# The down projections of a two-layer encoder on one core: sixteen instead of twelve of 22 k blocks as Strassen products

## The chip, the core and the metric

The kernel runs on one core of a Trainium2 chip. A core has five engines with a queue of instructions each: TensorE (PE, matmuls; PEld is its weight load), VectorE (DVE), ScalarE (ACT), GpSimd (POOL), and SyncE (SP), which issues the DMAs. They wait for each other by semaphores only. The metric is the device time of one execution in microseconds; three runs of the kernel before took 1592.32 to 1599.11, median 1592.86.

## The reference, cut to what matters

Two layers, each a token mixer, a cross-attention and a SwiGLU feed-forward; each of the three adds to the stream and normalises it.

```python
D_MODEL, SEQ, FFN_HIDDEN = 1024, 512, 2816

def swiglu(x, w_gu, w_down):
    gate, up = jnp.split(x @ w_gu, 2, axis=-1)
    return (jax.nn.silu(gate) * up) @ w_down

# in each layer, last
ff = swiglu(x, ffn_w_gu[layer], ffn_w_down[layer])
x = layer_norm(DEEPNORM_ALPHA * x + ff, ln_g[layer, 2], ln_b[layer, 2])
```

The change touches `(...) @ w_down` alone: 512 tokens by 2816 hidden features times 2816 by 1024.

## The kernel before, in words

**Three matmuls for one.** All is float32, but the matmuls run on float32r operands. Each operand is split into a high part (a cast on ACT) and a low part (the value minus the high part, on DVE or POOL), and a product is three matmuls: high by high, high by low, low by high. For weights the parts are `whi` and `wlo` (`chunk`, L131; `pair`, L543), for the hidden features `hi`/`lo`, and `fh`/`fl` for sums of them.

**The feed-forward** (`ffn`, L454). `fast_units` (L370) makes the 22 blocks of 128 hidden features, `raws[0]` to `raws[21]`, each 128 features by 512 tokens. `split` (L462) makes `hi` and `lo` of one. `fast_down` (L503) multiplies them by the down weights, in two ways that add into the same result:

- *Direct* (`mul`, L525): k blocks 0 to 9 in five pairs. One weight row of 128x1024 holds two k blocks by 512 output features; for one pair and one of the four token blocks that is 6 matmuls of 128x512. For the first half of the output features this is 120 matmuls into the four `pj` banks, ahead of the products; for the second half 120 matmuls behind them (L677 on).
- *Strassen* (L533 to L666): k blocks 10 to 21 in two halves `K[0]`, `K[1]` of six, cut by c into three groups of two. Tokens, output features and k are cut in two, and seven products p1 to p7 of sums and differences take the place of eight. A step is one (p, c): 12 matmuls of 128x512 (L661). Before it stands its preparation (`prep`, L601): a difference of weight rows (`diff`, L557), the split of it (`pair`), a sum of hidden blocks (`sums`, L579, tiles `sr`, `s3`), and its split (`tokens` L563, `whole` L572). `pair` of p3 and p2 and the sum `s3` of p7 are POOL's, the other sums, differences and low parts DVE's, the casts ACT's.

**What sets the order.** The steps are p1 and p5 in turn for each c; then p6, p3 and p7, each for all c; then p4 and p2 in turn for each c. `queue` holds the preparations in that order, with a step number; `upto` emits them some steps ahead of the matmuls. A layer that records the program then settles the order on each engine. Tiles come from rings: `raw` has 2 buffers, `whi`/`wlo` 5, `fh`/`fl` 6, `s3` 2. An operation that writes a tile waits until the reader of the buffer's last content is done. The tiles that hold the transposed stream (`mxh`, `mxl` here) serve as store for the weight rows b12 and b22 while the products run.

**The end of it.** When the two banks of a token half are done, `add` (L515) adds them to x on DVE; then `norm` (L303) normalises a token block: on DVE statistics, two passes of 512 columns twice, with a square root by POOL between. The output goes to the next layer or out.

Of the kernel before, what the change touches and what calls it, by code (L numbers as in the profile page):

```python
# [10 lines left out]
F32 = mybir.dt.float32  # L11
# [35 lines left out]
class Trunk:  # L47
# [406 lines left out]
    def ffn(self, l):  # L454
        nc, a = self.nc, self.a
        parts, raws = [], []
        self.halves = []

        def slot(j, dt):
            return self.kvblk(dt) if 8 <= j < 16 else self.part(dt=dt)  # L460

        def split(pool, n):  # L462
            j = len(parts)
            hi = pool.tile([P, S], F32R, tag="hi", bufs=n, name=self.nm("hi"))
            lo = self.kvblk(F32R) if 10 <= j < 18 else self.part()
            self.split(raws[j][0], hi, lo, raws[j][1])
            parts.append((hi, lo))

        def act(j, g, u, sign):

            s = slot(j, F32)
            nc.scalar.activation(g[1], g[0], AF.Silu)
            nc.vector.tensor_tensor(s, g[1], u, ALU.mult)
            raws.append((s, sign))

        with self.phase("pre") as pre:
            with self.phase("gu") as pool:
                new = self.tiles(pool)
                first = self.tproj_halves([a["gu"][l, j] for j in (0, HB, 1, HB + 1)])
                T = self.fast_tokens(lambda t: pool.tile([P, 4, 256], F32R, tag=t, name=self.nm(t)))  # L480
                for j in range(2):
                    pg, pu = first[2 * j:2 * j + 2]
                    act(j, (pg, new("o", 2, w=1024)[:, :512]), pu, 1)

                def unit(j):
                    def raw():
                        r = []
                        for x in (j, HB + j):
                            p = (self.wp, pool)[j % 2]
                            r.append(p.tile([P, 1024], F32, tag="raw", bufs=2, name=self.nm("raw")))  # L490
                            nc.sync.dma_start(r[-1], a["gu"][l, x])
                        return r
                    return {"raw": raw, "tag": ("at", "pj")[j % 2],
                            "done": lambda o: act(j, (o[:, :512], o[:, :512]), o[:, 512:], -1)}

                ready = []
                two = lambda: [split(pre, 6) for _ in range(2)]
                load = lambda: ready.append(self.chunk(a["down"][l][0, len(ready)]))
                self.fast_units([unit(j) for j in range(2, HB)], T, new, [load, two, load, two, two])
            with self.phase("down") as pool:  # L500
                self.fast_down(l, raws, parts, lambda: split(pool, 4), ready, pool)

    def fast_down(self, l, raws, parts, split, ready, pool):  # L503

# [1 line left out]
        mm = nc.tensor.matmul  # L508
        wsrc, idx = a["down"][l], 3 * l + 2
        last = idx + 1 == self.stop  # L510
        K = [[raws[10 + 6 * h + k][0] for k in range(6)] for h in range(2)]
        tok = slice(0, 256), slice(256, 512)
        res = []

# [19 lines left out]
        with self.phase("fast") as fp:  # L534
            new = self.tiles(fp)
            xt = [self.xtp.tile([P, KB, S], F32R, tag=t, name=self.nm("m" + t)).rearrange("p k s -> p (k s)")
                  for t in ("xh", "xl")]
            home = [x[:, i * 1024:(i + 1) * 1024].bitcast(F32) for x in xt for i in range(4)] + [new("t", 1, w=1024)]
            b12, b22, tt = home[:3], home[3:6], home[6:]
            sr = [new(f"sr{c}", 1) for c in range(3)]  # L540
            w, f, row = {}, {}, {}

            def pair(key, src, eng=None):  # L543
# [10 lines left out]
            def fetch(dst, h, i):  # L554
                nc.sync.dma_start(dst, wsrc[h, i])
# [2 lines left out]
                nc.vector.tensor_tensor(out, x, y, ALU.subtract)  # L558

            def form():  # L560
                return new("fh", 6, dt=F32R), new("fl", 6, dt=F32R)

            def tokens(key, src):  # L563
                hi, lo = form()
# [22 lines left out]
                return lambda k: sr[c][:, tok[k]]  # L587

            def b11(c):
                row[c] = stream(0, 5 + c)  # L590
                pair(("p1", c), row[c])

            def b21(c):
                row[c] = stream(0, 8 + c)
                diff(tt[c], row[c], tt[c])

            def s3(c):
                row["s3", c] = new("s3", 2)
                sums(row["s3", c], block(0, c, 0), block(0, c, 1), ALU.subtract, nc.gpsimd)

            prep = {  # L601
# [12 lines left out]
                "p4": lambda c: [lambda: b21(c), lambda: pair(("p4", c), tt[c]), lambda: whole(c)],  # L614
                "p2": lambda c: [lambda: pair(("p2", c), row[c], nc.gpsimd)],
            }
            steps = [(p, c) for c in range(3) for p in ("p1", "p5")]
            steps += [(p, c) for p in ("p6", "p3", "p7") for c in range(3)]
            steps += [(p, c) for c in range(3) for p in ("p4", "p2")]
            rest = b22 + b12[:2]  # L620
            early = [lambda: ready.append(self.chunk(wsrc[0, 2])), split, lambda: ready.append(self.chunk(wsrc[0, 3])),
                     split, lambda: [fetch(b12[c], 1, 5 + c) for c in range(3)], split,
                     lambda: ready.append(self.chunk(wsrc[0, 4])), split]
            queue = [(0, g) for g in early]
            for s, (p, c) in enumerate(steps):
                queue += [(s, g) for g in prep[p](c)]
                if s == 1:
                    queue += [(s, lambda: [fetch(b22[c], 1, 8 + c) for c in range(3)])]
                if (p, c) == ("p4", 0):
                    queue += [(s, lambda: [fetch(r, 1, i) for i, r in enumerate(rest)])]  # L630
            queue += [(len(steps) + i, lambda i=i: pair(i, rest[i])) for i in range(5)]

            def upto(s):
                while queue and queue[0][0] <= s:
                    queue.pop(0)[1]()

            pj = [self.bank("pj") for _ in range(TB)]
            for i in range(5):
                while len(ready) <= i or len(parts) < 2 * i + 2:
                    queue.pop(0)[1]()  # L640
                for t in range(TB):
                    mul(pj[t], t, i, ready[i], i == 0)
                    queue.pop(0)[1]()
                if i == 1:
                    for t in range(TB):
                        x = pool.tile([P, D], F32, tag=f"x{t}", name=self.nm("x"))
                        nc.sync.dma_start(x, self.xd[t * P:(t + 1) * P, :])
                        res.append((x, self.sp.tile([P, 2, 6], F32, tag="st", bufs=4, name=self.nm("st"))))
# [3 lines left out]
            to = {"p1": (0, 0, True, False), "p5": (2, 1, True, False), "p6": (0, 1, True, False),  # L652
                  "p7": (2, 0, True, False), "p4": (2, 0, False, True), "p2": (0, 0, False, True)}
            for s, (p, c) in enumerate(steps):
                upto(s + (4 if s >= 15 else 3))
                for t in range(2):
                    for k in range(2):
                        (fh, fl), tk, wk = f[p, c][k], slice(t * P, (t + 1) * P), slice(k * 512, (k + 1) * 512)
                        hi, lo = w[p, c]
                        for n, (l_, r) in enumerate(((fh, hi), (fh, lo), (fl, hi))):  # L660
                            mm(out[p][t], l_[:, tk], r[:, wk], start=c == k == n == 0 and p in ("p1", "p5"),  # L661
                               stop=k == 1 and n == 2, skip_group_check=True)
                if c == 2 and p in to:
                    t0, h, first, done = to[p]
                    for t in range(2):
                        add(out[p][t], t0 + t, h, first, done)  # L666
            upto(len(steps) + 5)
        with self.phase("ln") as lp:
# [5 lines left out]
            else:  # L674
                xd = self.dp.tile([S, D], F32, tag="xd", bufs=2, name=self.nm("xd"))
                self.new_xt()
            for ts, turns in (((0, 1), ()), ((2,), (3,)), ((3,), (2,))):  # L677
                for i in range(5):
                    for t in ts:
                        mul((y + z)[t], t, i, w[i], False)  # L680
                    if i in turns and not last:
# [755 lines left out]
```

## Time and profile before

| What | us |
|---|---|
| median of three runs (lowest, highest) | 1592.86 (1592.32, 1599.11) |
| the profiled execution; its span from first to last instruction | 1595.57; 1593.9 |
| busy in the span: PE, DVE, ACT, POOL | 1561.3, 1163.3, 785.4, 262.1 |
| products of layer 0, from 707.90 to 766.70 | 58.8 |
| last matmul of layer 1's down projection begins; the span ends | 1585.47; 1593.9 |

The mean granted clock of PE is 0.996 of full speed. Times of rows are from the start of the span. A row of a timeline has the start, the time taken, engine, line, operation, tile written <- tiles read, shapes, the count of equal instructions in it, and in brackets the engine's idle time before it with what ended it. Layer 0's down projection lies at 676 to 796 us, layer 1's at 1468 us to the end.

### The profile page before, as it was taken

To read this page: it belongs to the slowest core of one execution; us is meant where nothing else is said; L and a number is where in the kernel's file an instruction comes from. 1 tells how busy PE (TensorE), PEld (TensorE's weight loads), DVE (VectorE), ACT (ScalarE), POOL (GpSimd) and SP (SyncE) were. 2 spreads that over 40 slices of the span, in tenths; PEclk is the share of its full clock that TensorE was granted. 3 is DMA by queue.
4 is the path that set the end of the run, shared out by engine and by line. 5 is a ranking of instruction groups with operands and counts; after the bars stand their busy time and mean duration, and the time that the engine had idled before them with its cause. 6 is when DMAs were issued, how large, how long until landed. Compare 5 with 4: busy or idle time off the path is not lost.

```text
span 1593.9 us, 24998 instructions
## 1 busy us (share of the span) xinstructions
PE 1561.3 (98%) x9668; PEld 1375.4 (86%) x9668; DVE 1163.3 (73%) x1892; ACT 785.4 (49%) x1465; POOL 262.1 (16%) x263
## 2 busy tenths in 40 slices
PE   8999999999999999999999999989999999999997
PEld 7877887898899999988898977767988999999886
DVE  4684445475499989898766588776745998988986
ACT  4684455244255555445245566663442655554450
POOL 0012000221220000014131144232212100000151
PEclk9999999999999999999999999999999999999999
DMA  5432343442333333353254433403413333333531
GB/s 166 141 98 75 101 145 126 171 135 76 134 120 119 106 101 103 103 211 93 80 181 132 131 88 93 132 27 119 146 53 146 119 120 103 104 103 102 198 93 66
DMA packets 59415, 185.89 MB, mean 117 GB/s; under 512 B 7680, under 2 KB 7840, under 8 KB 59296
## 3 DMA queue, kind: packets, MB, share of 16 engines
q1 hardware_dynamic: 59296, 184.30, 35.7%
q8 instruction: 76, 1.25, 0.3%
q14 instruction: 43, 0.35, 0.1%
HBM read 167.47 MB, written 12.60 MB: 113 GB/s over the span
## 4 chain that ended last, share of the span: by engine, by line
PE 35%; DVE 6%; ACT 3%; POOL 2%; DMA 2%; issue 2%; SPq 0%; POOLq 0%; DVEq 0%; ACTq 0%
PE pj L143 3%; PE pj L145 3%; PE pj L144 3%; PE at L661 3%; PE pj L416 2%; PE pj L417 2%; PE at L531 2%; PE pj L418 2%; PE pj L531 2%; PE at L416 2%; PE at L417 2%; PE at L418 2%; PE at L143 2%; PE at L144 2%; PE at L145 2%
## 5 line engine op out<-in xcount | busy, mean ns | idle before, releaser
L137 ACT CAST whi<-raw 128x1024 fp32r<-128x1024 f32 (+2 forms) x158 | 159.3, 1009 | 194.8 <-PE pj L144 67.2
L138 DVE TENSOR_TENSOR wlo<-raw,whi 128x1024 fp32r<-128x1024 f32 (+2 forms) x142 | 170.3, 1202 | 110.6 <-ACT whi L137 104.1
L143 PE MATMUL pj<-xh,whi 128*128 128x512 f32 (+1 forms) x640 | 228.0, 356 | 0.0
L145 PE MATMUL pj<-xh,wlo 128*128 128x512 f32 (+1 forms) x640 | 216.9, 339 | 0.6 <-DVE wlo L138 0.6
L144 PE MATMUL pj<-xl,whi 128*128 128x512 f32 (+1 forms) x640 | 216.5, 338 | 0.0
L397 ACT CAST whi<-sump 128x512 fp32r<-128x512 f32 x160 | 97.6, 621 | 113.3 <-issue 64.4
L143 PEld LDWEIGHTS pj<-xh,whi 128*128 128x128 f32 x640 | 120.7, 189 | 15.7 <-issue 5.2
L144 PEld LDWEIGHTS pj<-xl,whi 128*128 128x128 f32 x640 | 120.7, 189 | 14.7 <-issue 3.8
L145 PEld LDWEIGHTS pj<-xh,wlo 128*128 128x128 f32 x640 | 120.4, 188 | 14.8 <-DVE wlo L138 0.8
L401 DVE TENSOR_TENSOR wlo<-sump,whi 128x512 fp32r<-128x512 f32 x160 | 107.7, 688 | 13.3 <-ACT whi L397 13.1
L397 ACT CAST whi<-raw 128x512 fp32r<-128x512 f32 x120 | 72.2, 617 | 32.2 <-PE at L417 14.8
L581 POOL TENSOR_TENSOR s<-kv 128x256 f32<-128x256 f32 x12 | 14.6, 1235 | 439.5 <-DVE o L435 434.8
L401 DVE TENSOR_TENSOR wlo<-raw,whi 128x512 fp32r<-128x512 f32 x120 | 81.2, 688 | 0.5
L220 POOL TENSOR_SCALAR s<-s 128x1 f32<-128x1 f32 x56 | 26.0, 464 | 310.8 <-DVE s L306 167.9
L416 PE MATMUL at<-xh,whi 128*128 128x256 f32 x240 | 67.8, 283 | 2.6 <-DVE o L431 2.6
L416 PE MATMUL pj<-xh,whi 128*128 128x256 f32 x240 | 68.3, 285 | 1.3 <-DVE o L431 1.3
L417 PE MATMUL pj<-xl,whi 128*128 128x256 f32 x240 | 67.9, 283 | 0.0
L417 PE MATMUL at<-xl,whi 128*128 128x256 f32 x240 | 67.9, 283 | 0.0
L418 PE MATMUL at<-xh,wlo 128*128 128x256 f32 x240 | 67.8, 283 | 0.0
L138 POOL TENSOR_TENSOR wlo<-raw,whi 128x1024 fp32r<-128x1024 f32 x16 | 38.3, 2392 | 179.6 <-ACT whi L137 179.6
L418 PE MATMUL pj<-xh,wlo 128*128 128x256 f32 x240 | 67.8, 282 | 0.0
L143 PE MATMUL pj<-whi,part 128*128 128x512 f32 x144 | 59.5, 413 | 0.0
(396 smaller groups left out, 4849.5 us busy)
## 6 DMA issues: line engine op xcount, KB each, us to landing
raw<-gu SPq DMA_DIRECT2D x88, 512.0 KB
raw<-down SPq DMA_DIRECT2D x22, 512.0 KB
xd<-x SPq DMA_DIRECT2D x40, 256.0 KB
x<-xd SPq DMA_DIRECT2D x20, 512.0 KB
raw<-wk SPq DMA_DIRECT2D x16, 512.0 KB
raw<-wv SPq DMA_DIRECT2D x16, 512.0 KB
raw<-wq SPq DMA_DIRECT2D x16, 512.0 KB
raw<-wo SPq DMA_DIRECT2D x16, 512.0 KB
```

Source lines behind the costliest of these rows:

```text
L137: nc.scalar.copy(hi[:, :w], raw[:, :w])
L138: (eng or self.lo_eng).tensor_tensor(lo[:, :w], raw[:, :w], hi[:, :w].bitcast(F32), ALU.subtract)
L143: mm(out, lh, rh, start=first, stop=False)
L144: mm(out, lh, rl, start=False, stop=False)
L145: mm(out, ll, rh, start=False, stop=last)
L397: nc.scalar.copy(n[p, "w"][0], n[p])
L401: nc.vector.tensor_tensor(lo, n[p], hi.bitcast(F32), ALU.subtract)
L416: mm(out, hi[:, c], th[k], start=first, stop=False, skip_group_check=True)
L417: mm(out, hi[:, c], tl[k], start=False, stop=False, skip_group_check=True)
L418: mm(out, lo[:, c], th[k], start=False, stop=k == 3, skip_group_check=True)
L531: mm(bank, s[:, tk], w[:, c], start=first and j == n == 0, stop=j == 1 and n == 2, skip_group_check=True)
L661: mm(out[p][t], l_[:, tk], r[:, wk], start=c == k == n == 0 and p in ("p1", "p5"), stop=k == 1 and n == 2, skip_group_check=True)
```

## The change

Sixteen k blocks instead of twelve go through the seven products, so there are four groups c and 28 steps of 12 matmuls instead of 21. Six k blocks (0 to 5) stay direct, 72 matmuls ahead of the products and 72 behind, instead of 120 each. Their six splits are all made at the end of `fast_units`; four more that `fast_down` made are gone. `fh`/`fl` have 5 pairs of buffers instead of 6 and `s3` has one instead of two; there are four scratch tiles `t` of 1024 columns for the weight differences instead of one (two others were in `mxl`). All weights are read once, as before.

```diff
-                self.fast_down(l, raws, parts, lambda: split(pool, 4), ready, pool)
+                self.fast_down(l, raws, parts, ready, pool)
...
-        K = [[raws[10 + 6 * h + k][0] for k in range(6)] for h in range(2)]
+        K = [[raws[6 + 8 * h + k][0] for k in range(8)] for h in range(2)]
...
-            home = [x[:, i * 1024:(i + 1) * 1024].bitcast(F32) for x in xt for i in range(4)] + [new("t", 1, w=1024)]
-            b12, b22, tt = home[:3], home[3:6], home[6:]
-            sr = [new(f"sr{c}", 1) for c in range(3)]
+            home = [x[:, i * 1024:(i + 1) * 1024].bitcast(F32) for x in xt for i in range(4)]
+            home += [new(f"t{c}", 1, w=1024) for c in range(4)]
+            b12, b22, tt = home[:4], home[4:8], home[8:]
+            sr = [new(f"sr{c}", 1) for c in range(4)]
...
-                return new("fh", 6, dt=F32R), new("fl", 6, dt=F32R)
+                return new("fh", 5, dt=F32R), new("fl", 5, dt=F32R)
...
-                row["s3", c] = new("s3", 2)
+                row["s3", c] = new("s3", 1)
...
-            steps = [(p, c) for c in range(3) for p in ("p1", "p5")]
-            steps += [(p, c) for p in ("p6", "p3", "p7") for c in range(3)]
-            steps += [(p, c) for c in range(3) for p in ("p4", "p2")]
-            rest = b22 + b12[:2]
-            early = [lambda: ready.append(self.chunk(wsrc[0, 2])), split, lambda: ready.append(self.chunk(wsrc[0, 3])),
-                     split, lambda: [fetch(b12[c], 1, 5 + c) for c in range(3)], split,
-                     lambda: ready.append(self.chunk(wsrc[0, 4])), split]
+            steps = [(p, c) for c in range(4) for p in ("p1", "p5")]
+            steps += [(p, c) for p in ("p6", "p3", "p7") for c in range(4)]
+            steps += [(p, c) for c in range(4) for p in ("p4", "p2")]
+            rest = b22[:3]
+            early = [lambda: ready.append(self.chunk(wsrc[0, 2])), lambda: [fetch(b12[c], 1, 3 + c) for c in range(4)]]
...
-            for i in range(5):
-                while len(ready) <= i or len(parts) < 2 * i + 2:
+            for i in range(3):
+                while len(ready) <= i:
...
-            for ts, turns in (((0, 1), ()), ((2,), (3,)), ((3,), (2,))):
-                for i in range(5):
+            for ts, turns in (((0, 1), ()), ((2,), (2,)), ((3,), (2,))):
+                for i in range(3):
```

The order on POOL, layer 0, from the first `s3` (named `s_...`) to the last, before. `wlo` read from `mxh` or `mxl` is p3's low part; an `s3` is two rows.

```order
L581 TENSOR_TENSOR s_1349_7644<-kv_5788 128x256
L581 TENSOR_TENSOR s_1349_7644<-kv_5921 128x256
L581 TENSOR_TENSOR s_1354_7668<-kv_6052 128x256
L581 TENSOR_TENSOR s_1354_7668<-kv_6185 128x256
L546 TENSOR_TENSOR wlo_7576<-mxh_7211,whi_7575 128x1024
L546 TENSOR_TENSOR wlo_7598<-mxl_7212,whi_7597 128x1024
L581 TENSOR_TENSOR s_1359_7692<-kv_6316 128x256
L546 TENSOR_TENSOR wlo_7620<-mxl_7212,whi_7619 128x1024
L581 TENSOR_TENSOR s_1359_7692<-kv_6449 128x256
```

And in the same place in the changed kernel:

```order
L582 TENSOR_TENSOR s_1356_7666<-part_5260 128x256
L582 TENSOR_TENSOR s_1356_7666<-part_5393 128x256
L547 TENSOR_TENSOR wlo_7576<-mxl_7212,whi_7575 128x1024
L547 TENSOR_TENSOR wlo_7598<-mxl_7212,whi_7597 128x1024
L547 TENSOR_TENSOR wlo_7620<-mxl_7212,whi_7619 128x1024
L547 TENSOR_TENSOR wlo_7644<-mxl_7212,whi_7643 128x1024
L582 TENSOR_TENSOR s_1361_7690<-kv_5524 128x256
L582 TENSOR_TENSOR s_1361_7690<-kv_5657 128x256
L582 TENSOR_TENSOR s_1366_7714<-kv_5788 128x256
L582 TENSOR_TENSOR s_1366_7714<-kv_5921 128x256
L582 TENSOR_TENSOR s_1371_7738<-kv_6052 128x256
L582 TENSOR_TENSOR s_1371_7738<-kv_6185 128x256
```

Before, two `s3` were made ahead of everything and the third stood around the last `wlo` of p3; now one stands ahead, then the four `wlo` of p3, then the other three `s3`.

The order on DVE, layer 0, from the first `fl` of an `s3` to the second low part of p7, before. `x` is the stream, `mxh` holds b12.

```order
L155 SCALAR_TENSOR_TENSOR fl_7652<-s_1349_7644,fh_7651 128x512
L558 TENSOR_TENSOR mxl_7212<-raw_7715,mxl_7212 128x1024
L558 TENSOR_TENSOR mxl_7212<-raw_7763,mxl_7212 128x1024
L155 SCALAR_TENSOR_TENSOR fl_7676<-s_1354_7668,fh_7675 128x512
L519 SCALAR_TENSOR_TENSOR x_7306<-x_7306,at_7435 128x512
L546 TENSOR_TENSOR wlo_7648<-mxh_7211,whi_7647 128x1024
L519 SCALAR_TENSOR_TENSOR x_7309<-x_7309,at_7436 128x512
L155 SCALAR_TENSOR_TENSOR fl_7700<-s_1359_7692,fh_7699 128x512
L546 TENSOR_TENSOR wlo_7672<-mxh_7211,whi_7671 128x1024
```

In the changed kernel, from the first low part of p7 to the last `fl` of an `s3`; `t_...` is the scratch for p4's weights:

```order
L547 TENSOR_TENSOR wlo_7670<-mxh_7211,whi_7669 128x1024
L155 SCALAR_TENSOR_TENSOR fl_7650<-sr_1268_7220,fh_7649 128x512
L155 SCALAR_TENSOR_TENSOR fl_7674<-s_1356_7666,fh_7673 128x512
L547 TENSOR_TENSOR wlo_7694<-mxh_7211,whi_7693 128x1024
L559 TENSOR_TENSOR mxh_7211<-mxl_7212,mxh_7211 128x1024
L155 SCALAR_TENSOR_TENSOR fl_7698<-s_1361_7690,fh_7697 128x512
L559 TENSOR_TENSOR mxh_7211<-mxl_7212,mxh_7211 128x1024
L547 TENSOR_TENSOR wlo_7718<-mxh_7211,whi_7717 128x1024
L155 SCALAR_TENSOR_TENSOR fl_7722<-s_1366_7714,fh_7721 128x512
L547 TENSOR_TENSOR wlo_7742<-mxh_7211,whi_7741 128x1024
L559 TENSOR_TENSOR t_1261_7213<-raw_7761,t_1261_7213 128x1024
L155 SCALAR_TENSOR_TENSOR fl_7746<-s_1371_7738,fh_7745 128x512
```

Each `fl` of an `s3` now has the low parts and differences of p7 and the first of p4 between it and the next.

## Rows read from the trace of the kernel before

**Rows 1.** Page, busy us, share of span, instructions

```profile
PE 1561.3 (98%) x9668; PEld 1375.4 (86%) x9668; DVE 1163.3 (73%) x1892; ACT 785.4 (49%) x1465; POOL 262.1 (16%) x263
```

**Rows 2.** Stretch of the products, us; busy of PE, PEld, DVE, ACT, POOL; clock

```profile
722.40:760.10 37.70, 37.70 (x163) 30.35 (x162) 31.68 (x31) 19.53 (x25) 21.90 (x8) 1.00 0.34 98
```

**Rows 3.** Timeline of PE, starts of steps; start, us, line, out<-in

```profile
707.90 0.39 PE L661 MATMUL at<-whi,fh 128*128 128x512 f32 x1
...
730.30 0.40 PE L661 MATMUL at<-whi,fh 128*128 128x512 f32 x1
...
738.70 0.40 PE L661 MATMUL at<-whi,fh 128*128 128x512 f32 x1
...
766.70 0.40 PE L531 MATMUL at<-whi,hi 128*128 128x512 f32 x1
```

**Rows 4.** Timeline of DVE, layer 0

```profile
686.51 1.23 DVE L473 TENSOR_TENSOR part<-o 128x512 f32<-128x512 f32 x1
...
693.76 1.43 DVE L581 TENSOR_TENSOR sr<-kv,part 128x256 f32<-128x256 f32 x4
...
709.34 1.22 DVE L546 TENSOR_TENSOR wlo<-raw,whi 128x1024 fp32r<-128x1024 f32 x1
710.47 1.22 DVE L558 TENSOR_TENSOR mxl<-mxl 128x1024 f32<-128x1024 f32 x1
...
721.31 1.22 DVE L546 TENSOR_TENSOR wlo<-t,whi 128x1024 fp32r<-128x1024 f32 x1
722.44 0.68 DVE L519 SCALAR_TENSOR_TENSOR x<-x,at 128x512 f32<-128x512 f32 x1
...
724.24 2.83 DVE L558 TENSOR_TENSOR mxh<-mxl,mxh 128x1024 f32<-128x1024 f32 x1
...
734.37 2.89 DVE L155 SCALAR_TENSOR_TENSOR fl<-s,fh 128x512 fp32r<-128x512 f32 x1
...
744.73 1.28 DVE L155 SCALAR_TENSOR_TENSOR fl<-part,fh 128x512 fp32r<-128x512 f32 x2
...
753.17 1.23 DVE L558 TENSOR_TENSOR t<-raw,t 128x1024 f32<-128x1024 f32 x1 [6.03 <-DMA raw<-down]
...
756.71 3.44 DVE L546 TENSOR_TENSOR wlo<-t,whi 128x1024 fp32r<-128x1024 f32 x1
```

**Rows 5.** Timeline of POOL, layer 0

```profile
723.52 2.47 POOL L546 TENSOR_TENSOR wlo<-mxh,whi 128x1024 fp32r<-128x1024 f32 x1 [34.31 <-ACT whi L545]
...
733.33 3.39 POOL L546 TENSOR_TENSOR wlo<-mxl,whi 128x1024 fp32r<-128x1024 f32 x1
736.67 1.19 POOL L581 TENSOR_TENSOR s<-kv 128x256 f32<-128x256 f32 x1
744.01 7.77 POOL L546 TENSOR_TENSOR wlo<-raw,whi 128x1024 fp32r<-128x1024 f32 x2 [6.15 <-issue]
```

**Rows 6.** Timeline of ACT, the third s3

```profile
737.89 0.64 ACT L154 ACTIVATE fh<-s 128x512 fp32r<-128x512 f32 x1 [5.99 <-POOL s L581]
```

**Rows 7.** Timeline of DVE, the end

```profile
1570.58 0.69 DVE L521 TENSOR_TENSOR x<-x,at 128x512 f32<-128x512 f32 x1 [8.70 <-PE at L531]
...
1579.37 0.68 DVE L521 TENSOR_TENSOR x<-x,at 128x512 f32<-128x512 f32 x1
...
1585.90 0.69 DVE L521 TENSOR_TENSOR x<-x,at 128x512 f32<-128x512 f32 x1 [1.57 <-PE at L531]
...
1589.45 1.42 DVE L312 SCALAR_TENSOR_TENSOR x<-x,s,gb 128x512 f32<-128x512 f32 x2 [0.44 <-POOL s L221]
```

**Rows 8.** Timeline of PE around a long wait in layer 1

```profile
1054.53 1.12 PE L962 MATMUL at<-ident,p 128*128 128x128 f32 x4 [5.08 <-ACT p L953]
...
1055.87 0.63 PE L950 MATMUL at<-st,st 128*128 128x512 f32 x1
1056.30 0.63 PE L949 MATMUL at<-st,st 128*128 128x512 f32 x1
```

**Rows 9.** Stretch behind that wait

```profile
1054.50:1058.00 3.50, 3.47 (x12) 3.09 (x13) 2.84 (x7) 1.97 (x5) 0.00 (x0) 0.50 0.00 0
```

More of the change, by code (lines that the diff above doesn't have):

```diff
@@ L500, in ffn, with fast_down @@
             with self.phase("down") as pool:
-                self.fast_down(l, raws, parts, lambda: split(pool, 4), ready, pool)
-    def fast_down(self, l, raws, parts, split, ready, pool):
+                self.fast_down(l, raws, parts, ready, pool)
+    def fast_down(self, l, raws, parts, ready, pool):
         nc, a = self.nc, self.a
@@ L589, in b11 @@
             def b11(c):
-                row[c] = stream(0, 5 + c)
+                row[c] = stream(0, 3 + c)
                 pair(("p1", c), row[c])
             def b21(c):
-                row[c] = stream(0, 8 + c)
+                row[c] = stream(0, 7 + c)
                 diff(tt[c], row[c], tt[c])
             def s3(c):
-                row["s3", c] = new("s3", 2)
+                row["s3", c] = new("s3", 1)
                 sums(row["s3", c], block(0, c, 0), block(0, c, 1), ALU.subtract, nc.gpsimd)
@@ L627, in fast_down @@
                 if s == 1:
-                    queue += [(s, lambda: [fetch(b22[c], 1, 8 + c) for c in range(3)])]
+                    queue += [(s, lambda: [fetch(b22[c], 1, 7 + c) for c in range(4)])]
                 if (p, c) == ("p4", 0):
                     queue += [(s, lambda: [fetch(r, 1, i) for i, r in enumerate(rest)])]
-            queue += [(len(steps) + i, lambda i=i: pair(i, rest[i])) for i in range(5)]
+            queue += [(len(steps) + i, lambda i=i: pair(i, rest[i])) for i in range(3)]
             def upto(s):
@@ L654, in fast_down @@
             for s, (p, c) in enumerate(steps):
-                upto(s + (4 if s >= 15 else 3))
+                upto(s + (4 if s >= 20 else 3))
                 for t in range(2):
@@ L662, in fast_down @@
                                stop=k == 1 and n == 2, skip_group_check=True)
-                if c == 2 and p in to:
+                if c == 3 and p in to:
                     t0, h, first, done = to[p]
```

## The prediction

> **What bounds the kernel now.** I read the page's busy shares first, then the clock and busy time of the stretches of one down projection, then the engines' timelines through it, and last its end. TensorE is busy for 98% of the span [rows 1], and the reader is to see that this holds inside the down projection too: in the stretch in which the products are formed, PE is busy for 37.70 of 37.70 us at full granted clock, and VectorE for 31.68 [rows 2]. So before the change the matmuls set the pace: one step of a product (a product p for one c, 12 matmuls) takes 2.80 us, since step 0 starts at 707.90 and step 8 at 730.30 [rows 3], which is 0.233 us for a matmul.
>
> What counts is how far ahead of it the operands are. Step 8 (p6, c=2) gets its last operand at 721.31 + 1.22 = 722.53 [rows 4] and starts at 730.30: a lead of 7.8 us. Step 11 (p3, c=2) gets its last one from GpSimd at 733.33 + 3.39 = 736.72 [rows 5] and starts at 738.70 [rows 3]: a lead of 2.0 us. Three steps of p3 cost 5.8 us of lead. VectorE and GpSimd cause that together: a subtraction of 128x1024, 1.13 us apart on VectorE when it runs alone, took 2.83 us while GpSimd worked (724.24 until 727.07; GpSimd's ended at 725.99), and a `fl` of 0.68 us took 2.89 [rows 4, 5]. The kernel before stays PE-bound because 28 us of direct matmuls stand ahead of step 0, in which operands are made in advance.
>
> **The change, part by part.** All is worked out for layer 0; layer 1 does the same once more.
>
> *Matmuls.* Per layer 120 + 252 + 120 become 72 + 336 + 72: 12 fewer of 0.233 us, 2.8 us a layer, 5.6 us in all. This is certain, and all on the path. But 48 of the direct ones leave the front: step 0 comes 48 x 0.233 = 11.2 us earlier, at 696.7 on the old clock, and step s at 696.7 + 2.80 s, unless its operands are late. Steps 0 to 27 replace 0 to 20.
>
> *Preparation up to step 11 (p1, p5, p6 for four c).* VectorE starts on it when the last hidden block is done, at 686.51 + 1.23 = 687.7 [rows 4]. In its queue then stand 21 operations of 1024 columns (3 `wlo` of p1, since the first goes earlier, 4 of p5, 4 of p6, 8 differences of p1 and p6, 2 of p7 that come early), 12 of 512 (8 `fl`, 4 additions to x) and 26 of 256 (18 sums, 8 `fl`). The starts lie 1.13 us apart for 1024 columns (709.34, 710.47), 0.60 for 512 (two in 1.28, one is 0.68) and 0.34 for 256 (four in 1.43) [rows 4]: 23.7 + 7.2 + 8.8 = 39.7 us, so the last operand of step 11 is there at 727.4. PE wants it at 696.7 + 30.8 = 727.5. The lead, 7.8 us before, is used up just where GpSimd comes in. That the splits of the last four hidden blocks and two weight chunks leave this stretch is in the count; without them it would be some 5 us worse.
>
> *Preparation of steps 12 to 27 (p3, p7, p4, p2).* VectorE: 14 operations of 1024 (2 differences and 4 `wlo` of p7, 4 and 4 of p4), 20 of 512 (16 `fl`, 4 additions), 6 sums of 256: 15.8 + 12.0 + 2.0 = 29.8 us. GpSimd: 8 `wlo` (p3, p2) of 2.47 us and 6 halves of `s3` of 1.19 [rows 5]: 26.9 us. Together 56.7 us, for which PE leaves 772.3 - 727.4 = 44.9 us until step 27. The cost lies between two ends. If the engines ran beside each other, 29.8 us would fit and nothing would stall; if they excluded each other wholly, PE would be 11.8 us late. The nearest row is the same work for three c: from 722.44 to 760.15 VectorE did 11 operations of 1024, 18 of 512, and GpSimd 6 `wlo` and 2 halves, first and last in [rows 4, 5]: 12.4 + 10.8 + 14.8 + 2.4 = 40.4 us of work in 37.7 us. They hid 7% of it. At that ratio 56.7 us take 52.9, and step 27 is 8.0 us late.
>
> To this comes time in which neither works. `s3` now has one buffer for four c: s3(c+1) can't start on GpSimd until VectorE has done the `fl` of s3(c), which waits for ScalarE's `fh`; and GpSimd's queue has all four `wlo` of p3 ahead of s3(1). VectorE takes its work in order, so behind a waiting `fl` stand the `wlo` of p7 and the first difference of p4, and PE waits for these. Before, ScalarE already sat 5.99 us until the third `s3` was there [rows 6], covered by the lead. Three such links, with 0.64 us of `fh` and some 0.2 of handing over in each, are an estimate of 2.5 us. A layer loses 10.5 us here, 21.0 in both, between 0 and 14.3 a layer.
>
> The Trainium skill says in "SBUF — State Buffer", SBUF: two separate sides, that VectorE with two SBUF inputs and a GpSimd operation share a port pair that is held for the whole instruction, so that the loser blocks fully. The 2.83 and 2.89 us [rows 4] bear it out, the additions to x, which read PSUM, being the exception. By that rule alone hiding is close to nothing and a layer loses 14.3 us; by the rows' ratio 10.5. I take the ratio, since it has those additions in it.
>
> *Scratch, rings, DMA.* `fh`/`fl` go from 6 to 5 pairs; a step can then be prepared 4 ahead, 11.2 us, more than the lead that is left, so I count it at nothing (with longer leads it would cap them). The weight loads are as many as before. p2 streams its row through the two `raw` buffers, and VectorE sat 6.03 us for such a load [rows 4]; that wait is inside the 37.7 us, so it scales along.
>
> *The end.* The last direct matmuls fall from 120 to 72, 11.2 us, but the norms behind them don't shrink. In layer 1 the first addition is at 1570.58, tile 2's at 1579.37 and tile 3's at 1585.90, when its matmuls end; the last of its operations begins at 1589.45 and ends at 1590.87, and the span ends 3.0 us later [rows 7]. Two tiles take 8.8 us, the third 4.9 (of 6.5 until 1585.90, the rest is a wait for PE), the fourth 5.0. After, the first addition is 24 matmuls = 5.6 us earlier relative to the last step, and the chain runs through without the 1.6 us wait: 7.2 of the 11.2 us arrive, 4.0 don't. At the end of layer 0 the same norms stand ahead of the next projection, whose first half needs only two tiles: between 0 and 4.0, I take 2.0.
>
> *Sum.* -5.6 + 21.0 + 4.0 + 2.0 = +21.4 us. The profiled execution took 1595.57 us (span 1593.9 and 1.7 around it), so it would take 1617.0; the median of the runs is 1592.86, 2.7 lower, and so I forecast 1614.
>
> **The rivals.**
>
> *Full exclusion.* If every VectorE operation with two SBUF operands waits out GpSimd's (14.3 us a layer), the change is +29 us, 1622. For it: the 2.89 us row. Against it: 7% was hidden before.
>
> *The clock.* After PE had sat idle for 5.08 us, its granted clock was 0.50 (the 1.2 GHz level) and the next matmuls came 0.43 us apart until about 1060 [rows 8, 9], some 2.5 us lost. In the stage before nothing idles, so its clock stays 1.00 [rows 2]. A stall of 8 to 10 us a layer comes in pieces of a step, 1 to 5 us. One piece as long as that in each layer adds 5, two add 10: 1619 to 1624. Against it: while the operands set the pace a slower PE is partly hidden.
>
> *Not slower.* The operands stay ahead. It would need a lead of 7.7 us at step 11 (5.8 us lost for three steps of p3, 7.7 for four), and the s3 chain to hide too. For it: PE waits for nothing in the stage today, and VectorE has 6.03 us idle in it. Then the change is -5.6 + 4.0 + 2.0 = +0.4, 1593; with no cost at the ends, 1587. It is decided by whether step 11 still finds its operands some 8 us early; I count 0.1.
>
> **How the numbers follow.** Forecast, 1606 to 1619: 0.60. Full exclusion, about 1622: 0.16. The clock, 1619 to 1628: 0.11. Not slower, 1587 to 1600: 0.13. The range that leaves out some 2 in 10 is 1601 to 1626; the forecast's own is 1606 to 1619. 0.5% of the time, 8 us, is about what can be told from no change. The matmuls removed are worth 5.6 us, so faster by more than that needs luck elsewhere: 0.02. Within it: 0.11. Slower: 0.87.
>
> **What would show it.** PE's share of the stretch of products falls from 100% to near 88%, its waits being for `wlo` of GpSimd and VectorE and `fl` of VectorE, the first at p3 and none in p1, p5 or p6. The stretch from step 0 to the last step grows from 58.8 us to 78.4 + 10.5, about 89 (over 92 for full exclusion, 79 for no stall). GpSimd runs four `wlo` in a row, then `s3` halves more than 3.5 us apart from one c to the next. The time from the last step to the span's end falls by about 7 us. The forecast is wrong if PE's first waits are already at p1 or p5, if the stretch stays under 82 us, or if matmuls there come 0.43 us apart.

## The result and the profile after

The changed kernel takes 1615.53 us (median of 4 runs, 1611.43 to 1616.48); the kernel before, beside it, 1593.96 (4 runs, 1592.32 to 1599.11). The ratio is 1.0129, with a 95% interval of 1.0116 to 1.0142. The profiled execution took 1615.25 us, its span is 1613.5.

The page of after, busy us, share of the span, instructions; 24 matmuls fewer than in [rows 1], yet a span 19.6 us longer:

```profile
PE 1564.5 (97%) x9644; PEld 1372.8 (85%) x9644; DVE 1199.5 (74%) x1922; ACT 793.5 (49%) x1479; POOL 279.8 (17%) x271
```

Stretches of after: the products of layer 0, those of layer 1, and a piece of the second. Columns: stretch; its length, then busy of PE, PEld, DVE, ACT, POOL; granted clock, DMA share, GB/s:

```profile
698.80:785.10 86.30, 80.23 (x337) 62.32 (x336) 81.89 (x88) 40.53 (x52) 33.19 (x14) 1.00 0.28 91
1498.43:1586.10 87.67, 81.53 (x337) 63.63 (x336) 82.92 (x89) 39.57 (x51) 33.15 (x14) 0.98 0.22 78
1568.50:1576.50 8.00, 7.60 (x26) 6.07 (x27) 7.83 (x9) 3.19 (x6) 2.99 (x2) 0.79 0.54 199
```

PE no longer fills the stretch as it did in [rows 2]: VectorE does, 81.89 of 86.30 us. From the first to the last matmul of a product it is 86.1 us in layer 0 and 87.5 in layer 1 (before 58.6 and 58.3). 28 steps without a wait take 77.9 (a run below shows it), so the lateness is near 8 us in layer 0 and 9.5 in layer 1, 1.5 of the latter at a lower clock.

The timeline of PE in layer 0: step 0, step 11, then every wait of the products, and the first direct matmul behind them (start, us, what; in brackets idle time and what ended it):

```profile
698.80 0.40 PE L660 MATMUL at<-whi,fh 128*128 128x512 f32 x1
...
729.60 0.40 PE L660 MATMUL at<-whi,fh 128*128 128x512 f32 x1
...
732.97 0.51 PE L660 MATMUL at<-wlo,fh 128*128 128x512 f32 x1 [0.17 <-POOL wlo L547]
...
742.84 0.50 PE L660 MATMUL at<-whi,fl 128*128 128x512 f32 x1 [0.94 <-DVE fl L155]
...
752.30 0.51 PE L660 MATMUL at<-whi,fh 128*128 128x512 f32 x1 [1.31 <-ACT fh L154]
...
756.18 0.50 PE L660 MATMUL at<-whi,fh 128*128 128x512 f32 x1 [0.57 <-ACT fh L154]
...
757.21 0.51 PE L660 MATMUL at<-whi,fl 128*128 128x512 f32 x1 [0.30 <-DVE fl L155]
...
769.31 0.50 PE L660 MATMUL pj<-whi,fl 128*128 128x512 f32 x1 [2.76 <-DVE fl L155]
...
785.11 0.39 PE L531 MATMUL at<-whi,hi 128*128 128x512 f32 x1
```

Steps 0 to 11 (p1, p5, p6) run without a wait. The first two are in p3, the next three in p7, and the longest in p4 at c=1, the step that begins at 765.2 (66.4 us behind step 0). GpSimd in the same stretch (the first row is the first of the four `wlo` of the second row, by itself):

```profile
727.99 4.93 POOL L547 TENSOR_TENSOR wlo<-mxl,whi 128x1024 fp32r<-128x1024 f32 x1 [41.81 <-ACT whi L546]
727.99 13.11 POOL L547 TENSOR_TENSOR wlo<-mxl,whi 128x1024 fp32r<-128x1024 f32 x4 [41.81 <-ACT whi L546]
743.46 3.33 POOL L582 TENSOR_TENSOR s<-kv 128x256 f32<-128x256 f32 x2 [2.36 <-DVE fl L155]
748.27 3.32 POOL L582 TENSOR_TENSOR s<-kv 128x256 f32<-128x256 f32 x2 [1.47 <-DVE fl L155]
753.05 2.42 POOL L582 TENSOR_TENSOR s<-kv 128x256 f32<-128x256 f32 x2 [1.46 <-DVE fl L155]
...
765.58 5.95 POOL L547 TENSOR_TENSOR wlo<-raw,whi 128x1024 fp32r<-128x1024 f32 x2 [3.77 <-ACT whi L546]
```

And VectorE, whose long operations are those beside GpSimd's. Its first row is the last operand of step 11; the `fl` of 728.62 that follows it belongs to step 12:

```profile
727.68 0.68 DVE L155 SCALAR_TENSOR_TENSOR fl<-sr,fh 128x512 fp32r<-128x512 f32 x1
...
729.22 1.43 DVE L582 TENSOR_TENSOR sr<-part,sr 128x256 f32<-128x256 f32 x4
731.20 0.69 DVE L519 SCALAR_TENSOR_TENSOR x<-x,at 128x512 f32<-128x512 f32 x1 [0.55 <-PE at L660]
731.81 4.46 DVE L155 SCALAR_TENSOR_TENSOR fl<-sr,fh 128x512 fp32r<-128x512 f32 x2
...
738.76 3.42 DVE L547 TENSOR_TENSOR wlo<-mxh,whi 128x1024 fp32r<-128x1024 f32 x1
...
744.44 1.76 DVE L559 TENSOR_TENSOR mxh<-mxl,mxh 128x1024 f32<-128x1024 f32 x1
747.50 0.69 DVE L155 SCALAR_TENSOR_TENSOR fl<-s,fh 128x512 fp32r<-128x512 f32 x1 [1.30 <-ACT fh L154]
...
752.28 0.69 DVE L155 SCALAR_TENSOR_TENSOR fl<-s,fh 128x512 fp32r<-128x512 f32 x1 [1.28 <-ACT fh L154]
...
766.41 2.85 DVE L155 SCALAR_TENSOR_TENSOR fl<-part,fh 128x512 fp32r<-128x512 f32 x1
```

Two kinds of loss can be read here. VectorE is held up by GpSimd: the `fl` at 766.41 takes 2.85 us instead of 0.68 while GpSimd makes two `wlo` from 765.58, and the 2.76 us wait of PE at 769.31 ends when it does. And the chain of the one `s3` buffer: GpSimd waits 1.46 to 2.36 us for VectorE's `fl`, VectorE 1.3 for ScalarE's `fh`, and PE's waits at 752.30 and 756.18 are for that `fh`.

The end of after, and the longest wait of PE at the start of layer 1 (us in total, times, longest):

```profile
1602.62 0.40 PE L531 MATMUL at<-whi,part 128*128 128x512 f32 x1
```

```profile
1603.05 0.69 DVE L521 TENSOR_TENSOR x<-x,at 128x512 f32<-128x512 f32 x1
...
1609.13 1.42 DVE L312 SCALAR_TENSOR_TENSOR x<-x,s,gb 128x512 f32<-128x512 f32 x2 [0.44 <-POOL s L221]
```

```profile
PE at L322 <- DVE x L312: 2.4, 1, 2.4
```

The addition to token block 3 now comes straight out of VectorE's queue, without the wait for PE that stood at it in [rows 7].

*The difference as a sum (profiled executions).* From the last matmul of the products to the end of the span it was 36.2 us and is 27.6: 8.6 of the 11.2 us of direct matmuls that are gone arrive. From the last one of layer 0 to the first direct matmul of layer 1 it was 701.8 and is 693.5: 8.3 arrive. With 11.1 and 11.0 us less from the first direct matmul to the products, 27.5 and 29.1 more in them, and 2.0 that the unchanged program ahead of layer 0's down projection took longer in this execution: 2.0 - 11.1 + 27.5 - 8.3 - 11.0 + 29.1 - 8.6 = 19.6 us, 1613.5 less 1593.9. The 8.3 at the boundary of the layers is the least steady of these: e6 below is the same as before at that place and took 699.9 there, and against it only 6.4 arrive.

### The profile page after: what moved, and what is told of

It reads as the page before. It is cut to its first block, busy times and chain, and to the rows that moved or that the text cites. A ratio compares the mean times of both kernels' runs of the same rounds, so it can differ in the third digit from the quotient of the medians.

```text
span 1613.5 us, 25004 instructions
## 1 busy us (share of the span) xinstructions
PE 1564.5 (97%) x9644; PEld 1372.8 (85%) x9644; DVE 1199.5 (74%) x1922; ACT 793.5 (49%) x1479; POOL 279.8 (17%) x271
## 5 line engine op out<-in xcount | busy, mean ns | idle before, releaser
L138 DVE TENSOR_TENSOR wlo<-raw,whi 128x1024 fp32r<-128x1024 f32 (+2 forms) x138 | 166.9, 1210 | 115.0 <-ACT whi L137 106.9
L137 ACT CAST whi<-raw 128x1024 fp32r<-128x1024 f32 (+2 forms) x154 | 155.0, 1007 | 182.8 <-PE pj L144 71.8
L397 ACT CAST whi<-raw 128x512 fp32r<-128x512 f32 x120 | 72.1, 617 | 31.8 <-issue 14.3
L401 DVE TENSOR_TENSOR wlo<-raw,whi 128x512 fp32r<-128x512 f32 x120 | 80.9, 685 | 0.4
L582 POOL TENSOR_TENSOR s<-part 128x256 f32<-128x256 f32 x4 | 7.1, 1790 | 426.5 <-DVE o L431 426.5
L660 PE MATMUL at<-whi,fh 128*128 128x512 f32 x160 | 63.3, 397 | 3.8 <-ACT fh L154 3.8
```

The costliest lines, as they stand in the source:

```text
L137: nc.scalar.copy(hi[:, :w], raw[:, :w])
L138: (eng or self.lo_eng).tensor_tensor(lo[:, :w], raw[:, :w], hi[:, :w].bitcast(F32), ALU.subtract)
L397: nc.scalar.copy(n[p, "w"][0], n[p])
L401: nc.vector.tensor_tensor(lo, n[p], hi.bitcast(F32), ALU.subtract)
```

## The experiments

"Late" is how much PE lost inside the products of a layer: the time by which a matmul's start lay more than 0.233 us behind the last one's, summed over the matmuls that were clearly late (by some 0.04 us or more). Each ratio is to runs of before on the same chip; the rows come from different chips, so they are compared by their ratios.

| kernel | median us (lowest, highest; runs) | ratio, 95% interval | products, layers 0 / 1 | late |
|---|---|---|---|---|
| changed | 1615.53 (1611.43, 1616.48; 4) | 1.0129 (1.0116, 1.0142) | 86.1 / 87.5 | 8.0 / 9.5 |
| e1 | 1602.01 (1600.59, 1603.66; 4) | 1.0049 (1.0034, 1.0064) | 81.1 / 80.9 | 3.0 / 3.0 |
| e2 | 1606.84 (1605.14, 1607.80; 4) | 1.0077 (1.0062, 1.0092) | 83.5 / 83.5 | 5.5 / 5.4 |
| e3 | 1597.26 (1594.72, 1599.23; 10) | 1.0020 (1.0010, 1.0030) | 77.9 / 77.9 | 0 / 0 |
| e4 | 1610.09 (1609.31, 1611.85; 4) | 1.0100 (1.0085, 1.0115) | 86.1 / 87.5 | as changed |
| e5 | 1593.45 (1592.74, 1596.56; 11) | 0.9990 (0.9981, 0.9998) | 77.9 / 77.9 | 0 / 0 |
| e6, from before | 1594.13 (1593.02, 1595.52; 10) | 0.9991 (0.9982, 1.0000) | 58.6 / 58.3 | 0 / 0 |
| e7 | 1612.41 (1610.61, 1613.88; 4) | 1.0102 (1.0086, 1.0117) | 86.5 / 86.2 | 8.3 / 8.3 |
| e8 | 1592.15 (1589.94, 1598.62; 9) | 0.9978 (0.9966, 0.9990) | 77.9 / 77.9 | 0 / 0 |
| e9 | 1597.45 (1595.70, 1603.03; 10) | 1.0022 (1.0011, 1.0032) | 78.9 / 79.1 | 1.0 / 1.1 |
| e10 | 1621.19 (1619.06, 1622.09; 4) | 1.0164 (1.0149, 1.0179) | 90.0 / 91.0 | 12.1 / 13.0 |
| e11 | 1608.80 (1605.46, 1612.65; 4) | 1.0089 (1.0070, 1.0108) | 85.1 / 85.1 | 6.9 / 7.0 |
| e12, from before | 1593.82 (1589.48, 1597.77; 11) | 0.9992 (0.9981, 1.0004) | 58.6 / 58.3 | 0 / 0 |

Spans say less than the products: the first direct matmul of layer 0, behind a program that none of these kernels changes, starts anywhere from 675.3 to 678.8 us in these profiles.

**e1: the low parts of p3 and p2 go from GpSimd to VectorE.**

```diff
-                "p3": lambda c: [lambda: pair(("p3", c), b22[c], nc.gpsimd),
+                "p3": lambda c: [lambda: pair(("p3", c), b22[c]),
...
-                "p2": lambda c: [lambda: pair(("p2", c), row[c], nc.gpsimd)],
+                "p2": lambda c: [lambda: pair(("p2", c), row[c])],
```

> The low parts of p3 and p2 go from GpSimd to VectorE, 8 per layer; the rest is as in the changed kernel. Theory A (VectorE and GpSimd shut each other out, so their work adds up): GpSimd loses 8 x 2.47 = 19.8 us, VectorE gains 8 x 1.13 = 9.0, the sum falls by 10.8 us a layer, and only the three links of s3 still stall PE. The stretch of products falls from 86 to 88 us to about 82, the time by 9 to 12 us to about 1605. Rival B (they run beside each other and VectorE alone is too full): VectorE gets 9 us more, the stretch grows to about 95 us, the time to about 1630. Rival C (only the s3 chain stalls): the stretch loses 1 to 2 us, 1612.

**e2: the `s3` sums go from GpSimd to VectorE.**

```diff
-                sums(row["s3", c], block(0, c, 0), block(0, c, 1), ALU.subtract, nc.gpsimd)
+                sums(row["s3", c], block(0, c, 0), block(0, c, 1), ALU.subtract)
```

> The differences s3 of p7 go from GpSimd to VectorE, 8 halves per layer; the rest is as in the changed kernel. Theory A: the waits in p7 (about 4 us a layer, 4.8 us from one s3 to the next in the trace) go, those for the low parts of p3 and p2 stay: the stretch is 82 to 84 us, the time about 1607. Rival B (VectorE too full): 8 x 0.34 = 2.7 us more for VectorE, the stretch grows to 89 us, 1619. Rival C (only the s3 chain stalls): all waits go, the stretch is 78.2 us, 1598.

**e3: both.**

> Both moves: in the products GpSimd does nothing. Theory A: VectorE has 29.8 + 9.0 + 2.0 = 41 us for steps 12 to 27, PE leaves 44.9: no step waits, the stretch is 78.2 us, and the time is that of the kernel before, less 5.6 us of matmuls, plus what the ends lose (2.6 and 2.9 us by the trace of after): about 1594. Rival B (VectorE alone too full): stretch over 95 us, 1630.

Each part takes away its share, in layer 0 5.0 and 2.5 us of the 8.0, and both together all of it. In e3 VectorE has 11.8 us more work of its own in each layer (8 of 1.13 and 8 of 0.34), and nothing is late. Its stretch of layer 0, columns as above:

```profile
699.00:777.00 78.00, 78.00 (x337) 63.09 (x336) 77.18 (x104) 42.41 (x53) 0.00 (x0) 1.00 0.25 87
```

PE 78.00 of 78.00, VectorE 77.18, GpSimd nothing: VectorE alone just keeps up. That is theory A's result in the products of all three, and rules out that VectorE's amount of work was the limit. The times fit it less closely: e1 came 3 us under the 1605 expected and e3 3 us above the 1594. It does not yet tell whether GpSimd's *running* or the *waiting for its results* cost the time; e10 does.

**e6: the edits of e3 in the kernel before**, a control.

> The kernel before with the same edit as e3_all: low parts of p3 and p2 and the s3 sums on VectorE, GpSimd idle in the products. Theory A: TensorE set the pace there already, so taking the GpSimd work away buys only lead: stretch of the products 58.5 us as before, lead of p3 at c=2 above 4 instead of 2.0 us, time 1594 within 2. So the gain of 18 us of e3_all over the changed kernel is the stall alone and not a gain that any kernel would get. Rival B (GpSimd's work costs time wherever it stands): 4 to 8 us under before, 1586 to 1590. Rival C (VectorE becomes too full): stretch above 62, above 1600.

The products stay at 58.6 and 58.3 us, the time within 0.2% of before: theory A. The lead of step 11 (p3, c=2), 2.0 us before, is 7.6 here and buys nothing: GpSimd's work costs nothing where the lead covers it.

**e10: e3, and GpSimd works for nobody.** `s3` is written over `sr` of the same c, and the tile that becomes free is GpSimd's scratch.

```diff
                 (eng or nc.vector).tensor_tensor(lo, src, hi.bitcast(F32), ALU.subtract)
+                if isinstance(key, tuple) and key[0] in ("p2", "p3"):
+                    for k in range(2):
+                        nc.gpsimd.tensor_tensor(idle, hi[:, :512].bitcast(F32), hi[:, 512:].bitcast(F32), ALU.subtract)
```

> As e3_all (VectorE does all of the preparation, nothing late, stretch 77.9 us, 1597), with a buffer of its own for each s3, and with GpSimd work that nobody needs: behind the cast of each step of p3 and p2 it subtracts two halves of the high part, 512 columns, twice, into a scratch tile. No operand comes from GpSimd, so this measures what its mere running costs VectorE. Between 1.19 us for 256 columns and 2.47 for 1024, 512 take some 1.6, so 16 of them are 26 us a layer, as much as GpSimd had to do in the changed kernel. Theory A (the two engines exclude each other, as the stretched operations of VectorE showed): VectorE's subtractions beside them take 2 to 3.5 us instead of 1.22; VectorE's 41 us of work and 26 of GpSimd's at 7% hidden are 62 us where PE leaves 45, stretch 88 to 96, time 1615 to 1632. Rival B (the stall came from waiting for GpSimd's results, not from its running): VectorE's operations stay at 1.22, stretch 78 to 79, 1597 to 1599.

Theory A, in the products and in the time. GpSimd (its first operation by itself, then the first eight together), VectorE and ScalarE of e10, layer 0:

```profile
727.12 6.54 POOL L551 TENSOR_TENSOR s<-whi 128x512 f32<-128x512 f32 x1 [258.38 <-ACT whi L547]
727.12 17.92 POOL L551 TENSOR_TENSOR s<-whi 128x512 f32<-128x512 f32 x8 [258.38 <-ACT whi L547]
...
775.62 3.56 POOL L551 TENSOR_TENSOR s<-whi 128x512 f32<-128x512 f32 x2 [3.26 <-ACT whi L547]
```

```profile
730.95 1.22 DVE L548 TENSOR_TENSOR wlo<-mxl,whi 128x1024 fp32r<-128x1024 f32 x1
...
733.23 0.98 DVE L155 SCALAR_TENSOR_TENSOR fl<-sr,fh 128x512 fp32r<-128x512 f32 x1 [0.73 <-ACT fh L154]
...
737.37 2.31 DVE L548 TENSOR_TENSOR wlo<-mxl,whi 128x1024 fp32r<-128x1024 f32 x1
739.60 2.89 DVE L586 TENSOR_TENSOR sr<-part,sr 128x256 f32<-128x256 f32 x2
742.41 2.90 DVE L586 TENSOR_TENSOR sr<-part 128x256 f32<-128x256 f32 x2
745.24 1.21 DVE L548 TENSOR_TENSOR wlo<-mxh,whi 128x1024 fp32r<-128x1024 f32 x1
...
775.71 2.32 DVE L548 TENSOR_TENSOR wlo<-raw,whi 128x1024 fp32r<-128x1024 f32 x1
```

```profile
742.52 0.63 ACT L154 ACTIVATE fh<-sr 128x512 fp32r<-128x512 f32 x1 [5.28 <-DVE sr L586]
```

Beside GpSimd a subtraction of 1024 columns takes 2.31 us, and two of 256 take 2.89 instead of 0.75; as soon as GpSimd is done, at 745.04, it is 1.21 again. It does not begin with GpSimd's first operation: beside that one VectorE's subtractions still took 1.22, and it was GpSimd's that took 6.54 us, until 1.2 us after VectorE first stood idle (732.50 to 733.23). No operand comes from GpSimd, and none of VectorE's operations there waits for a semaphore of GpSimd's, so the engines do not wait for each other by semaphores only. Yet PE is 12 to 13 us late in a layer, some 10 of it in waits and the rest at a lower clock.

GpSimd could also have held up ScalarE, since a buffer of `whi` is not written again until GpSimd has read it. The trace shows no such wait: of ScalarE's waits in the products of e10 none ends with GpSimd, in either layer. Its 5.28 us ahead of the `fh` that PE waits longest for are for VectorE's stretched sums.

**e7: each `s3` in a buffer of its own; GpSimd keeps its work.**

```diff
-                row["s3", c] = new("s3", 1)
+                row["s3", c] = sr[c]
```

> The changed kernel with a buffer of its own for each s3 (it is written over sr of the same c, which p6's operands have left free by then); GpSimd keeps its work. Theory A (the single s3 buffer is a part of the stall, 2.5 us of 10.5 in each layer; the rest is work on VectorE and GpSimd that excludes each other): the waits in p7 shrink, the stretch falls from 86.1 and 87.5 to 83 to 85, time 1609 to 1613. Rival B (only the sum of the work of both engines counts): stretch 86 to 87.5, 1614 to 1616. Rival C (the chain of the single buffer is nearly all of it): stretch under 80, under 1603.

The products came out at 86.5 and 86.2, which is B's number, but not B's way; the time, 1612.41, lies in A's range. Without the buffer to wait for, GpSimd takes sums ahead of the last `wlo` of p3. GpSimd and PE of e7:

```profile
738.95 1.72 POOL L582 TENSOR_TENSOR sr<-part 128x256 f32<-128x256 f32 x1
740.62 2.32 POOL L582 TENSOR_TENSOR sr<-kv 128x256 f32<-128x256 f32 x2
742.91 3.32 POOL L547 TENSOR_TENSOR wlo<-mxl,whi 128x1024 fp32r<-128x1024 f32 x1
```

```profile
746.28 0.80 PE L660 MATMUL at<-wlo,fh 128*128 128x512 f32 x1 [3.94 <-POOL wlo L547]
746.87 0.63 PE L660 MATMUL at<-whi,fl 128*128 128x512 f32 x1
747.30 0.63 PE L660 MATMUL at<-whi,fh 128*128 128x512 f32 x1
```

All waits in p7 are gone, but p3 waits 3.94 us for that `wlo`, and the matmuls behind it come 0.43 us apart. Of the 8.3 us late, 6.0 are waits (8.0 in the changed kernel) and 2.3 the lower clock. So PE waits 2 us less without the chain, though with another order on GpSimd too, and the clock takes that back in layer 0. By the ratios e7 is 4 us under the changed kernel; of that, the products explain 0.9, and the rest is not placed.

**e9: e1 with the edit of e7.** Here no `wlo` of GpSimd can get in the way.

> As e1_lows (low parts of p3 and p2 on VectorE, s3 sums still on GpSimd), but each s3 has a buffer of its own, written over sr of the same c. In e1_lows PE was 3.0 us late in a layer, all of it in p7. Theory A (those 3 us are the chain of the single s3 buffer: GpSimd's sum waits for VectorE's low part, which waits for ScalarE's cast): nothing is late in p7, stretch of the products 77.9 to 78.5 us, time 1596 to 1598. Rival B (GpSimd's sums are late for another reason, their length of 2.4 us or VectorE work that they hold up): stretch 80 to 81 as in e1_lows, 1601 to 1603.

Late falls from 3.0 to 1.0 us, all waits in p7 are gone, and the median falls by 4.6 us: theory A, short of its last 1.0 (two waits in p3 for `fl` and `fh`).

**e11: e2 with the edit of e7.**

> As e2_s3 (s3 sums on VectorE, low parts of p3 and p2 still on GpSimd), but each s3 has a buffer of its own. In e2_s3 PE was 5.5 us late in a layer, about 2 of it in p7. Theory A (VectorE and GpSimd hold each other up; what the single buffer cost there is the part in p7): stretch 81 to 83, time 1602 to 1606. Rival B (only the single buffer made anything late): 78 to 79, 1597. Rival C (the buffer plays no part here, since VectorE itself writes it in order): 83.5 as e2_s3, 1607.

85.1 against 83.5 in e2: A's number missed, and C (the buffer plays no part where VectorE fills it itself) is nearest. The waits in p7 did go, but in both kernels PE then waits for the same `fl` of p4 at c=2, behind a difference of VectorE's that GpSimd's `wlo` stretches to 3.43 us in e2 and 3.31 in e11 (1.22 alone). That `fl` ends 73.6 us behind step 0 in e2 and in e11, so what PE does not wait for earlier it waits for there: 2.7 us in one piece in e11, where e2 has 1.7. Behind the longer wait the clock fell, and that is the 1.5 us between the two.

**e4 and e5: the last direct matmuls token block by token block**, in the changed kernel and in e3.

```diff
-            for ts, turns in (((0, 1), ()), ((2,), (2,)), ((3,), (2,))):
+            for ts, turns in (((0,), ()), ((1,), ()), ((2,), (2,)), ((3,), (2,))):
```

> In the last direct part token blocks 0 and 1 are taken one after the other instead of together; the rest is as in the changed kernel. Theory (the norms on VectorE set the end): the first addition comes after 18 matmuls instead of 30, 2.8 us earlier, so that the end comes 1.5 to 2.8 us earlier and the wait of 2.4 us for the transposes after layer 0 goes too: 1611, and the time from the last step to the end falls from 27.6 to about 26. Rival (the end is set by the last matmuls): no change, 1615.

> The changed kernel with VectorE doing the low parts of p3 and p2 and the s3 sums (as in e3_all), and with the last direct matmuls taken token block by token block (as in e4_tail). Theory A (a stall of the products and a loss at the ends are the only two costs, and they are independent): stretch of the products 77.9 us in each layer as in e3_all, last step to span's end 27.2 as in e4_tail against 27.6, and the wait of the first matmuls of layer 1 for x 1.3 instead of 2.4; so 2 to 5 us under e3_all (the difference of e4_tail to the changed kernel was 5), 1592 to 1595, the same as the kernel before. Rival B (what e4_tail gained was noise): 1597, as e3_all.

By the ratios e4 is 4.6 us under the changed kernel and e5 4.8 under e3, with the same products in each pair. The times are those expected, but not the place: from the last step to the end of the span it was 27.6 before the edit and is 27.2 in e4 and e5, where e4 expected about 26. That is only 0.4 us. From the last step of layer 0 to the first direct matmul of layer 1 the eight kernels with the old order took 692.6 to 693.9 us, e4 690.5 and e5 692.3: a part of the gain is there, 0.3 to 3.4 us, and the rest is not placed. In e5 PE's wait there became 2.9 us for `xl` and `xh`, not the 1.3 expected.

**e8: e5, with both transposes of the new stream that stood in the direct part (one behind the last pair of block 2, one behind that of block 3) in block 3**, behind its pairs 0 and 2.

```diff
-            for ts, turns in (((0,), ()), ((1,), ()), ((2,), (2,)), ((3,), (2,))):
+            for ts, turns in (((0,), ()), ((1,), ()), ((2,), ()), ((3,), (0, 2))):
```

> As e5_both, with the transposes of token blocks 0 and 2 both behind the direct matmuls of block 3 instead of block 2's ahead of them, at the end of each layer's down projection. Theory A (what is left at the boundary of the layers is a wait of the first matmuls of layer 1 for the norm of the last blocks, 1.3 us): the wait shrinks, 0.5 to 2 us under e5_both. Rival B (the wait only moves to where the transposes now stand): same as e5_both within 1 us.

PE's wait at the boundary falls from 2.9 to 1.7 us and the median by 1.3, on the same chip: theory A, though the intervals of e5 and e8 overlap. This is the best version, 0.1 to 0.3% under before.

**e12: the kernel before with the edits of e5**, a control (pairs 3 and 2 stay its `turns`).

> Control for e5_both: the kernel before with the same two edits (GpSimd's part of the products on VectorE, and the last direct matmuls token block by token block). Theory A (the end of the kernel before hides its norms: the last token block's additions wait 1.57 us for PE whatever stands ahead, so finishing blocks 0 and 1 one after another moves nothing): last step to span's end 36.2 as before, time 1593 to 1595, and e5_both is 0 to 2 us under it. Rival B (the edit shortens the end or the boundary of the layers here too): 1590 to 1592, and e5_both has no gain of its own.

From the last step to the end 36.3 us, as before, and 0.9992 of before: theory A. Against it e5's 0.9990 is no gain; the 5.6 us of matmuls that the change removes are, even without any stall, taken up by the ends (of 11.2 us of direct matmuls less at each, the profile of e5 is shorter than that of e12 by 6.5 at the boundary and by 9.1 at the end).

## Why the prediction was right

The forecast was 1614 us with 1606 to 1619 as its own range; it came to 1615.53. Its terms:

- **Matmuls, -5.6: right.** 24 fewer, and 28 steps without a stall take 77.9 us (forecast 78.4 with the first direct one).
- **The lead used up at step 11: right.** Step 11 starts 30.8 us behind step 0, at 729.60, and its last operand, the `fl` of 727.68, ends at 728.36: a lead of 1.2 us (forecast: 0.1). PE's first wait is the `wlo` of p3, as forecast.
- **The stall, 10.5 a layer: right in kind, too large.** 8.0 and 9.5 were measured. The work of both engines for steps 12 to 27 runs from 727.99 to the last `fl` of VectorE at 777.02 + 2.57 = 779.59: 51.6 us for the 56.7 of work, with the waits of the chain in it, where the ratio and the chain gave 52.9 + 2.5. A part of what looked hidden was never there: half an `s3`, priced at 1.19 us, takes 0.74 at its shortest. The chain is worth 2.0 us (e9 against e1), forecast 2.5; the exclusion then, by difference, 6.0, forecast 8.0. The price of full exclusion (92 us, 14.3 a layer) is out.
- **Where the stall falls: not at the end of the work, as the sum had it.** All of it stands by 769.31, in p4 at c=1; step 27 begins at 782.3, 3.3 us behind the last `wlo`. So the sum of the work gives the size of the stall here but not its place. The forecast also named VectorE's `wlo` among PE's waits; there is none, and 1.9 of PE's 6.1 us of idle time in layer 0 are for ScalarE's `fh`, behind the chain.
- **The `fl`/`fh` pairs and the DMAs at nothing: bore out.** e3 runs 28 steps on the same five pairs and transfers with nothing late.
- **The ends, 4.0 and 2.0: 2.6 and 2.9.** The last norms do run through without a wait for PE. At the boundary 2.4 of the 2.9 us are a wait of PE for the normalised stream; the 2.9 is as unsteady as the 8.3 above (4.8 against e6).
- **The clock, a rival at 0.11: it came, small.** Only layer 1 lost 1.5 us to it, where the rival had 5 and more. Matmuls 0.43 us apart were also a sign that the forecast would be wrong; it showed in layer 1 for 3.3 us without changing the outcome.

So -5.6 + 17.5 + 2.6 + 2.9 = 17.4, and with the 2.0 us of scatter ahead of it 19.4, against 19.6 between the two spans and 21.4 forecast. The stall was 3.5 too high. That the median nonetheless came within 1.5 us of the forecast is in part luck: the medians lie 21.6 apart, and the 4 us above the 17.4 are the scatter of 2.0 and a difference between profiled and median executions, neither of which is in the forecast's sum. The page showed PE at 93% of the stretch, not 88%, since a matmul counts as busy longer (0.39 us) than it keeps the next one away (0.233).

The Trainium skill ("SBUF — State Buffer", SBUF: two separate sides) has VectorE with two SBUF inputs and a GpSimd operation that reads SBUF lock each other out for the whole instruction. The `fl` of 2.85 us at 766.41, which ends 0.55 us behind GpSimd's `wlo`, and e10 above all, bear that out operation by operation. Taken as "nothing is hidden" it would have given 14.3 us a layer; 8.0 were lost.

## What to carry to other kernels

Where one engine's queue feeds PE with a lead, read the lead at each step before moving work to the front or taking cover away: here a lead of 7.8 us at step 8 was part of what hid the shared work of VectorE and GpSimd, and the extra group, with 11 us less of direct matmuls ahead, used it up. Two engines that stretch each other's operations count nearly as one, with the sum of their work (here 51.6 us for 56.7); an elementwise operation that takes half the time on VectorE is not "free" on an idle GpSimd. And matmuls removed from a kernel's end pay only as far as the norms behind them are not already the longer chain.

## What the runs showed of the hardware that was not expected

- **A wait of 2.7 to 2.8 us sometimes takes PE to the lower clock.** Behind 2.76 us of idle time in layer 0 (769.31) the matmuls came 0.23 us apart; behind 2.75 in layer 1, at the same matmul, they slowed from the fifth on, to 0.43 apart, for 3.3 us, at a granted clock of 0.52 (the 1.2 GHz level). In e4 the same happened in the same two places; in e11 it slowed behind 2.73 and 2.72 us in both layers, and in e7 behind 3.94 at once. What decides it no run here shows. PE of after, layer 1; over the 8 us around it the granted clock is 0.79:

```profile
1568.90 0.50 PE L660 MATMUL pj<-whi,fl 128*128 128x512 f32 x1 [2.75 <-DVE fl L155]
...
1569.70 0.56 PE L660 MATMUL pj<-whi,fl 128*128 128x512 f32 x1
1570.06 0.63 PE L660 MATMUL pj<-whi,fh 128*128 128x512 f32 x1
1570.49 0.63 PE L660 MATMUL pj<-wlo,fh 128*128 128x512 f32 x1
...
1573.35 0.40 PE L660 MATMUL pj<-whi,fl 128*128 128x512 f32 x1
```

- **Both engines lose, and a VectorE without gaps goes first.** GpSimd's first `wlo` at 727.99 took 4.93 us (2.4 to 2.5 at best). VectorE's operations beside it, back to back until 730.65, took no longer than alone, and the `wlo` ended 2.3 us after that gap of VectorE's. GpSimd's first operation in e10 did the same. From then on VectorE's were stretched too, and GpSimd's other three `wlo` of p3 took 2.6 to 2.9 us. Half an `s3` took 1.65 to 1.73 us beside VectorE, 0.74 where it began in a gap.
- **Short operations of GpSimd hold VectorE up less.** Beside the 256-column halves, 1024 columns on VectorE took 1.76 us instead of 1.22; beside 1024-column ones 3.42.
